# The last half step's raw weight quarters get six tiles of their own, and its token sums get narrower tiles

## The chip, the cores and the metric

The kernel runs on one core of one Trainium2 chip. The metric is device time of one execution in microseconds (us). A core has TensorE (PE, with PEld for its weight loads), VectorE (DVE), ScalarE (ACT), GpSimd (POOL) and SyncE (SP); here SP does nothing but issue DMAs, and POOL issues some DMAs between its vector operations. Each engine takes its instructions in the order in which they were written for it, and an instruction whose inputs or buffer are not ready holds up all that stand behind it on that engine.

## The reference

A backbone of two layers over 512 latent tokens and 256 context tokens of width 1024. Each layer is: a half SwiGLU feed-forward step, a token mixer (neighbourhood attention, then windowed attention), and a second half step. Each part is modulated, gated and closed by a layer norm. All four half steps compute the same formula, with a hidden width of 2816:

```
def swiglu(u, w_in, w_out):
    a, v = jnp.split(u @ w_in, 2, axis=-1)
    return (jax.nn.silu(a) * v) @ w_out

def ffn_sublayer(h, shift, scale, gate, w_in, w_out, g, b):
    y = swiglu(modulate(h, shift, scale), w_in, w_out)
    return layer_norm(ALPHA * h + FFN_RES * gate * y, g, b)
```

In the last half step of the last layer the context tokens are no longer needed, so it runs on the 512 latent tokens alone. That is the half step of this change; the code calls it `1b`.

## The kernel before

**Precision.** A matrix product is made of three fp32r matmuls: each operand is split into a high part and a low part (high x high, low x high, high x low; `mm3`, lines 163, 165 and 166). A weight tile of 128 x 512 comes from memory raw (`wr`), ACT copies it into its high part `wh` (line 102), and POOL or DVE subtracts to get the low part `wl` (line 104). High and low parts of a half step's weights live in a ring of eight tiles each (`RING = 8`), so a new pair can be written only when TensorE is done with the pair eight back.

**A half step.** The hidden width is cut into eleven chunks of 256. A chunk has two weight units of w_in (128 columns of a and 128 of v each) and one unit of w_out. In the middle eight chunks a w_in unit is not multiplied plainly: `seven` multiplies its four quarters in Strassen's manner with seven products instead of eight, over pairs of 128-column token blocks. For that the unit is read as four raw quarters, `wr..00`, `wr..01`, `wr..10` and `wr..11` (a11, a12, a21, a22; `raw_quarter`, line 94 issues the load on SP). POOL makes four sums of them, `S_1` to `S_4` (line 645), each of 128 x 512. Seven pairs of high and low parts follow: for a11, a12 and a22 straight from the quarters (`wh_a`, `wl_a`), for the four sums `wh_s`, `wl_s`. In half step `1b` (where the code's `nb` is 2) DVE makes the low parts of a11, a12, a22 and S_3, POOL those of S_2, S_1 and S_4.

The token side of the products is prepared once per half step: `sums` makes three sums of token blocks for each of four rows and writes their high and low parts to the tiles `T..h` and `T..l` (lines 606 and 607). TensorE then writes the products `p0` to `p6` to PSUM banks; DVE combines them (line 675, tiles `y`), ACT applies silu and copies the high part of the result (`gh`, line 679), and DVE makes its low part (`gl`). The banks of `p5` and `p6` come free with the `gl` operations.

**The w_out unit lags.** A chunk's w_out unit (`lagging`) is multiplied one unit later than its own chunk: TensorE runs the second unit of chunk n, the first unit of chunk n+1, the w_out product of chunk n (`pd`, eight blocks of 128 outputs, accumulated into `z` by DVE at line 504), the second unit of chunk n+1, and so on. There are seven such w_out products in `1b` within the stretch of seven-product units. The low part of a lagging weight is made without a vector subtraction: ACT writes minus the high part (line 108) and a DMA issued by POOL adds the raw weight from memory on top (line 109, `wl_0b` to `wl_3b`).

**Tiles.** Before the change, quarters and the raw tiles of lagging units come from one ring of five (`tag="wr"`, `RAWS = 5`, 2 KB per partition each), in program order. The tiles `T` and two of the `y` tiles are 384 columns wide in every half step, and in `1b` only 256 of them are used (`n2`).

**Order.** The kernel is written with a scheduler that puts the instructions of each engine in an order from its own model of times, when the kernel is built; then the order is fixed. A change to which tile an instruction waits for can therefore move instructions on any engine.

Of the kernel before, what the change touches and what calls it, by code (L numbers as in the profile page):

```python
# [8 lines left out]
F32 = mybir.dt.float32  # L9
F32R = mybir.dt.float32r  # L10
# [7 lines left out]
P = 128  # L18
# [14 lines left out]
RAWS = 5  # L33
# [4 lines left out]
def hybrid_kernel(ctx: ExitStack, tc: tile.TileContext, h0, cc, crow, wmod, wmodt, bmod, lnp, wst,  # L38
# [4 lines left out]
    wp = ctx.enter_context(tc.tile_pool(name="wp", bufs=1))  # L43
# [5 lines left out]
    def bank(tag, nm):  # L49
        return pp.tile([P, 512], F32, tag=tag, name=nm, bufs=banks[tag])  # L50

    def t2(nm, tag="t2"):
        return tp.tile([P, 512], F32, tag=tag, name=nm, bufs={"t2": 6, "ln": 2, "sl": 2}[tag])
# [35 lines left out]
    def flat_or_tiles(t, src):  # L89
        return t[:] if len(src.shape) == 2 else t[:].rearrange("p (k c) -> p k c", c=P)  # L90

    def raw_quarter(src, nm):
        raw = wp.tile([P, 512], F32, tag="wr", name=f"wr{nm}", bufs=RAWS)
        loaded[0] = nc.sync.dma_start(flat_or_tiles(raw, src), src)
        return raw

# [14 lines left out]
    ph, phase_of, slabs_kept = {}, [None, ExitStack()], [SLABS]  # L111
# [397 lines left out]
    def ffn(nm, groups, gt, mid, post, units=(), opened={}, head=None, apart=None):  # L509
# [45 lines left out]
        nb = groups[-1][1] // 256  # L555
        n2 = nb * P
# [13 lines left out]
        def op(eng, out, a, b, o):  # L570
            a, b = [half(y[0], y[1]).bitcast(F32) if isinstance(y, tuple) else as_half(y) for y in (a, b)]
            x = eng.tensor_tensor(out=as_half(out), in0=a, in1=b, op=o)
            if paced:
                behind(x, last_gate[0] if opened else last[0])
# [7 lines left out]
        def sums(j, pool=False):  # L582

            if not paced:
                if not kept_x:
                    kept_x.extend(bank(t, f"x{nm}_{t}") for t in "to")
                b = kept_x[j % 2]
                x1 = (kept_x[0][:, 0:n2], kept_x[1][:, 0:n2], kept_x[1][:, 0:n2], t2(f"x{nm}_{j}_0")[:, 0:n2])[j]
                x2 = (b[:, 256:512] if j < 2 else b[:, 0:256])
                x2s.append(x2)  # L590
            else:
                x1, x2 = [t2(f"x{nm}_{j}_{i}")[:, 0:n2] if pool else bank("s", f"x{nm}_{j}_{i}")[:, 0:n2] for i in range(2)]
            eng = nc.gpsimd if pool else nc.vector
            x3 = t2(f"x{nm}_{j}_2")[:, 0:n2]
            k = j + 4
            op(eng, x1, (uh[j], 1), (uh[j], 0), ALU.subtract)
            op(eng, x1, x1, (ul[j], 1), ALU.add)
            op(eng, x1, x1, (ul[j], 0), ALU.subtract)
            op(nc.gpsimd, x3, (uh[k], 1), (uh[j], 1), ALU.subtract)
            op(nc.gpsimd, x3, x3, (ul[k], 1), ALU.add)  # L600
            op(nc.gpsimd, x3, x3, (ul[j], 1), ALU.subtract)
            op(eng, x2, (uh[k], 1), x1, ALU.subtract)
            op(eng, x2, x2, (ul[k], 1), ALU.add)
            for i, x in enumerate((x1, x2, x3)):
                hi, lo = [ph["T"].tile([P, 384], F32R, tag=f"T{i}{j}{y}", name=f"T{nm}_{i}_{j}{y}", bufs=1)[:, 0:n2] for y in "hl"]
                nc.scalar.copy(hi, x)
                y = nc.vector.tensor_tensor(out=lo, in0=x, in1=hi.bitcast(F32), op=ALU.subtract)
                if paced:
                    behind(y, last_gate[0] if opened else last[0])
                ts[i][j] = [as_half(hi), as_half(lo)]  # L610
# [26 lines left out]
        def quarters(u):  # L637

            src = wst[u].rearrange("p (k c) -> p k c", c=256)
            a11, a12, a21, a22 = [raw_quarter(src[:, h * 4:h * 4 + 4, m * P:m * P + P], f"{u}_{m}{h}")  # L640
                                  for m in range(2) for h in range(2)]

            def tt(n, a, b, o):
                t = t2(f"S{u}_{n}")
                nc.gpsimd.tensor_tensor(out=t[:], in0=a[:], in1=b[:], op=o)  # L645
                return t

            def pair(n, src):
                hi, lo = ring_pair(f"{u}_{n}")
                split_w(hi, lo, src, eng=nc.vector if nb == 2 and n in ("a11", "a12", "a22", "s3") else nc.gpsimd,  # L650
                        y=evacuated[0])
                return hi, lo

            out = [pair("a11", a11), pair("a12", a12)]
            s1 = tt(1, a21, a22, ALU.add)
            s2 = tt(2, s1, a11, ALU.subtract)
            out += [pair("s2", s2), pair("s1", s1)]
            s4 = tt(4, a12, s2, ALU.subtract)
            s3 = tt(3, a11, a21, ALU.subtract)
            return out + [pair("s4", s4), pair("s3", s3), pair("a22", a22)]  # L660

        def seven(un, u, gh, gl):
# [17 lines left out]
                op(half(gl, h), as_half(v), half(gh, h).bitcast(F32), ALU.subtract)  # L680

            sa, sb = [t2(f"y{un}_{i}", "sl")[:, 0:n2] for i in range(2)]
            va, vb = [ph["T"].tile([P, 384], F32, tag=f"y{i}", name=f"y{i}{un}", bufs=2 - i)[:, 0:n2] for i in range(2)]
            nc.scalar.copy(va, product(0, b11))
            tick()
            op(sa, product(1, b21), va)
# [109 lines left out]
        u = wpos[0]  # L796
# [766 lines left out]
```

## Time and profile before

| what | value |
|---|---|
| median of three runs | 2715.3 us (2712.52 to 2730.1) |
| the profiled execution: time, span | 2717.3 us, 2715.5 us |
| busy share of the span: PE, PEld, DVE, ACT, POOL | 97%, 88%, 67%, 44%, 61% |
| granted TensorE clock, mean of the profiled execution | 0.993 |
| the stretch of seven-product units of `1b` | about 2400 to 2632 us of the span |

Busy time is the time in which an instruction of the engine ran; waiting is not in it. Rows of a timeline give the start and the duration in us, the engine, the line of the source, the operation with its written and read tiles, and in brackets how long the engine had been idle before it and what ended that wait. The chain of waits goes back from the last instruction, at each step to what released it. A name's buffer number is left out in the profile, so `S` stands for all four sums, `wr` for any raw quarter, and `pd1b` for the eight blocks of the w_out product of `1b`. In rows of order, the number in a name is the weight unit: in the text below 138 is the second unit of a chunk, 139 that chunk's w_out unit, 140 the first unit of the next chunk, 141 its second.

### The profile page before, as it was taken

The numbers are of one execution on the slowest core, as the hardware profiler recorded it, in microseconds if no ns is written. First come the engines' busy times: TensorE is split into PE (matmuls) and PEld (weight loads), VectorE is DVE, ScalarE is ACT, GpSimd is POOL, SyncE is SP. The second block draws the span as 40 slices with busy tenths as digits, with TensorE's granted clock in tenths as the row PEclk, the third lists the DMA queues.
The fourth block names the chain that finished last, engine by engine and source line by source line (L and its number), as shares of the span: only waits on it lengthen the run. The fifth ranks groups of instructions, "written<-read, shape, count | busy, mean of one in ns | idle before, by whom it ended". The sixth has DMA issues, their size and how long they took to land.

```text
span 2715.5 us, 47718 instructions
## 1 busy us (share of the span) xinstructions
PE 2624.7 (97%) x16858; PEld 2399.9 (88%) x16858; DVE 1828.9 (67%) x4268; ACT 1207.2 (44%) x2505; POOL 1659.6 (61%) x1515
## 2 busy tenths in 40 slices
PE   8999999999999999999999999999999998899997
PEld 5899998888888899999998889999988776899997
DVE  4977778775545686555565776666677767677765
ACT  5334343266455453443433534343337655544542
POOL 4786766455433666867574668676645545667762
PEclk9999999999999999999999999999999999999998
DMA  9367465422211122454543225556642111235551
GB/s 333 100 178 208 137 166 142 147 78 80 59 59 52 50 80 67 129 136 119 133 127 99 75 78 148 143 137 189 178 139 63 32 32 47 71 98 129 143 142 55
DMA packets 294606, 310.85 MB, mean 114 GB/s; under 512 B 27744, under 2 KB 192864, under 8 KB 293344
## 3 DMA queue, kind: packets, MB, share of 16 engines
q1 hardware_dynamic: 277952, 278.31, 33.9%
q0 software_dynamic: 16128, 29.37, 6.4%
q8 instruction: 133, 2.18, 0.3%
q14 instruction: 105, 0.86, 0.1%
q10 hardware_dynamic: 288, 0.14, 0.0%
HBM read 299.87 MB, written 12.25 MB: 115 GB/s over the span
## 4 chain that ended last, share of the span: by engine, by line
PE 83%; DVE 9%; ACT 3%; DMA 2%; issue 2%; POOL 1%; DVEq 0%; SPq 0%; ACTq 0%; POOLq 0%
PE pd1a L163 2%; PE pd1a L165 2%; PE pd1a L166 2%; PE pd0b L163 2%; PE pd0b L165 2%; PE pd0b L166 2%; PE pd0a L163 2%; PE pd0a L165 2%; PE pd0a L166 2%; DVE z L504 1%; PE wo L911 1%; PE pd1b L163 1%; PE o L911 1%; DMA wr<-in_wst_dram 1%; PE pd1b L165 1%
## 5 line engine op out<-in xcount | busy, mean ns | idle before, releaser
L104 POOL TENSOR_TENSOR wl<-wr,wh 128x512 fp32r<-128x512 f32 x200 | 261.1, 1323 | 149.8 <-ACT wh L102 80.0
L104 POOL TENSOR_TENSOR wl_s<-S,wh_s 128x512 fp32r<-128x512 f32 x240 | 316.3, 1355 | 41.6 <-ACT wh_s L102 41.2
L102 ACT CAST wh_s<-S 128x512 fp32r<-128x512 f32 x256 | 155.7, 621 | 413.5 <-POOL S L645 143.2
L645 POOL TENSOR_TENSOR S<-wr,wr 128x512 f32<-128x512 f32 x128 | 173.4, 1355 | 205.4 <-DMA wr<-in_wst_dram 177.7
L212 DVE CUSTOM_DVE_ANT_0 jk<-wt,cb 128x512 f32<-128x512 f32 x360 | 244.4, 679 | 22.9 <-DMA wt<-in_wmodt_dram 18.8
L104 POOL TENSOR_TENSOR wl_a<-wr,wh_a 128x512 fp32r<-128x512 f32 x144 | 190.6, 1371 | 16.4 <-ACT wh_a L102 13.0
L102 ACT CAST wh_a<-wr 128x512 fp32r<-128x512 f32 x192 | 118.7, 622 | 151.3 <-PE pd1b L165 20.9
L102 ACT CAST wh<-wr 128x512 fp32r<-128x512 f32 x200 | 121.2, 617 | 101.2 <-DMA wr<-in_wst_dram 19.5
L504 DVE SCALAR_TENSOR_TENSOR z<-pd0b,gt,z 128x256 f32<-128x256 f32 (+1 forms) x168 | 97.0, 594 | 43.7 <-PE pd0b L166 41.7
L504 DVE SCALAR_TENSOR_TENSOR z<-pd1a,gt,z 128x512 f32<-128x512 f32 (+1 forms) x150 | 88.2, 604 | 31.5 <-PE pd1a L166 24.1
L920 POOL TENSOR_SCALAR p<-p,l 128x512 f32<-128x512 f32 x64 | 44.3, 694 | 104.7 <-DVE l L1034 93.5
L504 DVE SCALAR_TENSOR_TENSOR z<-pd0a,gt,z 128x512 f32<-128x512 f32 (+1 forms) x160 | 94.0, 612 | 16.9 <-PE pd0a L166 16.6
L645 POOL TENSOR_TENSOR S<-wr,S 128x512 f32<-128x512 f32 x64 | 90.4, 1413 | 3.5
L645 POOL TENSOR_TENSOR S<-S,wr 128x512 f32<-128x512 f32 x64 | 90.3, 1411 | 3.1
L920 POOL TENSOR_SCALAR pw<-pw,l 128x512 f32<-128x512 f32 (+1 forms) x64 | 42.6, 666 | 71.1 <-DVE l L1260 41.3
L340 POOL TENSOR_SCALAR z<-z,ag_None,ab_None 128x256 f32<-128x256 f32 (+1 forms) x69 | 53.0, 773 | 48.6 <-DVE uh L325 31.3
L1033 ACT ACTIVATE p<-s,m 128x512 f32<-128x512 f32 x64 | 43.9, 688 | 74.4 <-DVE m L1030 70.1
L326 DVE TENSOR_TENSOR ul<-ufl,uh 128x256 fp32r<-128x256 f32 (+1 forms) x88 | 55.7, 639 | 7.1 <-ACT uh L321 4.1
L319 ACT ACTIVATE ufl<-z,bi_None,sc_None 128x256 f32<-128x256 f32 (+1 forms) x77 | 48.1, 637 | 25.3 <-DVE z L489 24.7
L504 DVE SCALAR_TENSOR_TENSOR z<-pd1b,gt,z 128x512 f32<-128x512 f32 (+1 forms) x91 | 53.1, 617 | 9.0 <-PE pd1b L166 6.2
L163 PE MATMUL vn<-wh,uh 128*128 128x256 f32 x192 | 54.6, 284 | 1.0 <-DVE nq L863 0.6
L104 DVE TENSOR_TENSOR wl_a<-wr,wh_a 128x512 fp32r<-128x512 f32 x48 | 51.7, 1088 | 5.3 <-ACT wh_a L102 5.3
(1483 smaller groups left out, 10565.1 us busy)
## 6 DMA issues: line engine op xcount, KB each, us to landing
wr<-in_wst_dram SPq DMA_DIRECT2D x456, 256.0 KB
wt<-in_wmodt_dram SPq DMA_DIRECT2D x206, 256.0 KB
wr_0b<-in_wst_dram SPq DMA_DIRECT2D x47, 256.0 KB
wr_1b<-in_wst_dram SPq DMA_DIRECT2D x47, 256.0 KB
wr_2b<-in_wst_dram SPq DMA_DIRECT2D x47, 256.0 KB
wr_3b<-in_wst_dram SPq DMA_DIRECT2D x47, 256.0 KB
wm<-in_wmod_dram SPq DMA_DIRECT2D x8, 1024.0 KB
zspare<-in_wmodt_dram SPq DMA_DIRECT2D x30, 256.0 KB
```

Of the source, the lines that this page charges most:

```text
L102: nc.scalar.copy(hi[:], src[:])
L104: x = eng.tensor_tensor(out=lo[:], in0=src[:], in1=hi[:].bitcast(F32), op=ALU.subtract)
L163: behind(nc.tensor.matmul(ps, a[0], b[0], start=first, stop=False), in_front[0])
L165: nc.tensor.matmul(ps, a[0], b[1], start=False, stop=False)
L166: last_pe[0] = nc.tensor.matmul(ps, a[1], b[0], start=False, stop=last)
L212: x = nc.vector.tensor_tensor_reduce(out=junk[:], in0=w[:], in1=cb[st], scale=1.0, scalar=0.0, op0=ALU.mult, op1=ALU.add, accum_out=out[st])
L326: return hi, nc.vector.tensor_tensor(out=lo, in0=uv, in1=uo.bitcast(F32), op=ALU.subtract)
L340: nc.gpsimd.tensor_scalar(out=zs, in0=zs, scalar1=prm[2][:, d:d + 1], scalar2=prm[3][:, d:d + 1], op0=ALU.mult, op1=ALU.add)
L504: last[0] = nc.vector.scalar_tensor_tensor(out=zt(d, c0, c1), in0=pd, scalar=gt[:, d, st:st + 1], in1=zt(d, c0, c1), op0=ALU.mult, op1=ALU ...
L645: nc.gpsimd.tensor_tensor(out=t[:], in0=a[:], in1=b[:], op=o)
L911: last_pe[0] = nc.tensor.matmul(po[64 * h:64 * h + 64, :], t[h][0], t[h][1], start=i == 0, stop=i == len(terms) - 1)
L920: nc.gpsimd.tensor_scalar(out=p, in0=p, scalar1=r, scalar2=0.0, op0=ALU.mult, op1=ALU.add)
```

## The change

In half step `1b` alone, the quarters of the seven-product units no longer come from the ring of five: they take six tiles of their own, in the pool of the phase, and the ring of five is left to the w_out units (and to what comes before and after that stretch). The tiles `T` and `y` are allotted as wide as they are used (`n2`: 256 columns in `1b`, 384 in the others as before). No operation, shape or transfer is added or taken away.

```diff
-    def raw_quarter(src, nm):
-        raw = wp.tile([P, 512], F32, tag="wr", name=f"wr{nm}", bufs=RAWS)
+    def raw_quarter(src, nm, own=None):
+        if own is None:
+            raw = wp.tile([P, 512], F32, tag="wr", name=f"wr{nm}", bufs=RAWS)
+        else:
+            raw = own.tile([P, 512], F32, tag="wr", name=f"wr{nm}", bufs=6)
         loaded[0] = nc.sync.dma_start(flat_or_tiles(raw, src), src)
         return raw
...
-                hi, lo = [ph["T"].tile([P, 384], F32R, tag=f"T{i}{j}{y}", name=f"T{nm}_{i}_{j}{y}", bufs=1)[:, 0:n2] for y in "hl"]
+                hi, lo = [ph["T"].tile([P, n2], F32R, tag=f"T{i}{j}{y}", name=f"T{nm}_{i}_{j}{y}", bufs=1)[:] for y in "hl"]
...
-            a11, a12, a21, a22 = [raw_quarter(src[:, h * 4:h * 4 + 4, m * P:m * P + P], f"{u}_{m}{h}")
+            a11, a12, a21, a22 = [raw_quarter(src[:, h * 4:h * 4 + 4, m * P:m * P + P], f"{u}_{m}{h}",
+                                              ph["T"] if nb == 2 else None)
...
-            va, vb = [ph["T"].tile([P, 384], F32, tag=f"y{i}", name=f"y{i}{un}", bufs=2 - i)[:, 0:n2] for i in range(2)]
+            va, vb = [ph["T"].tile([P, n2], F32, tag=f"y{i}", name=f"y{i}{un}", bufs=2 - i)[:] for i in range(2)]
```

Outside `1b` the order of every engine is unchanged, and within it ACT's order is unchanged. POOL, SP, PE and DVE have instructions in other places. On POOL, between the sums of unit 140 and the low parts of unit 141, this stands before the change:

```order
L104 TENSOR_TENSOR wl140_s2_28315<-S140_2_28312,wh140_s2_28314 128x512
L104 TENSOR_TENSOR wl140_s1_28319<-S140_1_28310,wh140_s1_28318 128x512
L104 TENSOR_TENSOR wl140_s4_28327<-S140_4_28322,wh140_s4_28326 128x512
L109 DMA wl139_0b_28452<-in_wst_dram 128x512
L109 DMA wl139_1b_28459<-in_wst_dram 128x512
L109 DMA wl139_2b_28466<-in_wst_dram 128x512
L109 DMA wl139_3b_28473<-in_wst_dram 128x512
L645 TENSOR_TENSOR S141_1_28557<-wr141_10_28545,wr141_11_28547 128x512
L645 TENSOR_TENSOR S141_2_28559<-S141_1_28557,wr141_00_28541 128x512
L645 TENSOR_TENSOR S141_4_28569<-wr141_01_28543,S141_2_28559 128x512
L645 TENSOR_TENSOR S141_3_28571<-wr141_00_28541,wr141_10_28545 128x512
```

In the changed kernel POOL has the same eleven instructions in this order (the lines are three or four further down in its source):

```order
L107 TENSOR_TENSOR wl140_s2_28315<-S140_2_28312,wh140_s2_28314 128x512
L649 TENSOR_TENSOR S141_1_28557<-wr141_10_28545,wr141_11_28547 128x512
L107 TENSOR_TENSOR wl140_s1_28319<-S140_1_28310,wh140_s1_28318 128x512
L649 TENSOR_TENSOR S141_2_28559<-S141_1_28557,wr141_00_28541 128x512
L107 TENSOR_TENSOR wl140_s4_28327<-S140_4_28322,wh140_s4_28326 128x512
L649 TENSOR_TENSOR S141_4_28569<-wr141_01_28543,S141_2_28559 128x512
L649 TENSOR_TENSOR S141_3_28571<-wr141_00_28541,wr141_10_28545 128x512
L112 DMA wl139_0b_28452<-in_wst_dram 128x512
L112 DMA wl139_1b_28459<-in_wst_dram 128x512
L112 DMA wl139_2b_28466<-in_wst_dram 128x512
L112 DMA wl139_3b_28473<-in_wst_dram 128x512
```

The four sums of unit 141 have moved ahead of the four adding DMAs of unit 139, and between the low parts of unit 140. On SP, the loads of one chunk stand like this before the change:

```order
L94 DMA wr138_10_28139<-in_wst_dram 128x4x128
L94 DMA wr138_11_28141<-in_wst_dram 128x4x128
L94 DMA wr140_00_28294<-in_wst_dram 128x4x128
L94 DMA wr140_01_28296<-in_wst_dram 128x4x128
L94 DMA wr140_10_28298<-in_wst_dram 128x4x128
L94 DMA wr140_11_28300<-in_wst_dram 128x4x128
L94 DMA wr139_0b_28449<-in_wst_dram 128x512
L94 DMA wr139_1b_28456<-in_wst_dram 128x512
L94 DMA wr139_2b_28463<-in_wst_dram 128x512
L94 DMA wr139_3b_28470<-in_wst_dram 128x512
L94 DMA wr141_00_28541<-in_wst_dram 128x4x128
L94 DMA wr141_01_28543<-in_wst_dram 128x4x128
```

and in the changed kernel like this:

```order
L97 DMA wr138_10_28139<-in_wst_dram 128x4x128
L97 DMA wr138_11_28141<-in_wst_dram 128x4x128
L97 DMA wr140_00_28294<-in_wst_dram 128x4x128
L97 DMA wr140_01_28296<-in_wst_dram 128x4x128
L97 DMA wr139_1b_28456<-in_wst_dram 128x512
L97 DMA wr140_10_28298<-in_wst_dram 128x4x128
L97 DMA wr139_2b_28463<-in_wst_dram 128x512
L97 DMA wr139_3b_28470<-in_wst_dram 128x512
L97 DMA wr142_0b_28855<-in_wst_dram 128x512
L97 DMA wr140_11_28300<-in_wst_dram 128x4x128
L97 DMA wr141_00_28541<-in_wst_dram 128x4x128
L97 DMA wr141_01_28543<-in_wst_dram 128x4x128
```

The w_out loads have moved ahead of the last quarter of unit 140, the one of the next chunk's w_out unit (142) among them. On PE the eight blocks of a w_out product are taken in the order 0, 1, 2, 3, 4, the first matmul of 6, 5, the rest of 6, 7 instead of 0, 1, 2, 3, 6, 4, 5, 7; on DVE the accumulations follow that, and one of them moves behind a `gl` operation.

## The prediction

> **What bounds the kernel now.** I read the page first, for which engine fills the span, then the stretch of seven-product units by itself (its busy times, and its waits by engine), then the chain of waits inside it, and last the timelines of POOL, DVE and TensorE over one chunk.
>
> ```profile
> span 2715.5 us, 47718 instructions
> PE 2624.7 (97%) x16858; PEld 2399.9 (88%) x16858; DVE 1828.9 (67%) x4268; ACT 1207.2 (44%) x2505; POOL 1659.6 (61%) x1515
> ...
> 2400.00:2632.00 232.00, 228.19 (x1589) 212.11 (x1588) 167.78 (x282) 114.70 (x235) 167.54 (x131) 1.00 0.54 132
> ...
> PE pd1b L163 <- DVE gl1b L675: 3.8, 3, 2.0
> POOL S L645 <- DMA wr<-in_wst_dram: 36.4, 12, 7.5
> ACT wh_s L102 <- POOL S L645: 53.3, 18, 9.0
> ```
>
> TensorE fills 97% of the span. In the 232.0 us that the change touches it is busy for 228.19 at a granted clock of 1.00 (the columns are span, then PE, PEld, DVE, ACT, POOL, clock, DMA share, GB/s). The difference is 3.8 us, and the waits of TensorE there are the same 3.8 us: three waits of the w_out product for a `gl` operation. POOL waits 36.4 us for raw quarters and ACT 53.3 us for the sums made of them, but almost all of that lies beside a busy TensorE. So the most that this stretch can give is 3.8 us of 2715, or 0.14%.
>
> How the three waits come about is seen in the chain, here at the longest of them:
>
> ```profile
> 2421.80 10.12 DMA wr<-in_wst_dram
> 2432.07 1.28 POOL S L645
> 2433.42 1.30 POOL S L645
> 2434.97 0.30 issue
> 2435.27 0.61 ACT wh_s L102
> 2435.88 0.28 ACT gh1b L679
> 2436.19 0.43 DVE gl1b L675
> 2436.66 0.50 PE pd1b L163
> ```
>
> A raw quarter lands 10.12 us after its issue, POOL makes two sums, ACT copies their high parts, and only then comes the copy `gh`, which stands behind them in ACT's order though it needs no sum. With `gl` a PSUM bank comes free, and the w_out product goes on. The 10 us of the transfer cost TensorE 2.0 us here (the longest of the three).
>
> In the chunk that the rest of this text follows, the same link of the chain is this:
>
> ```profile
> 2486.46 8.51 DMA wr<-in_wst_dram
> ```
>
> **What the change takes away.** Two units fill eight quarters in a chunk. In the ring of five a quarter of unit 141 waits for tiles that w_out unit 139 still holds, so its load goes out only after ACT has made that unit's parts, at 2486.46 in that chunk, and lands 8.51 us later amid the four adding DMAs. With six own tiles the last two quarters of a unit take the tiles of the first two quarters of the unit before: `wr141_10` and `wr141_11` follow `wr140_00` and `wr140_01`, which are free when POOL has made S140_4 and S140_3 and DVE has made the low parts of those two quarters. That is about ten microseconds earlier, and ahead of the adding DMAs. The sums of 141 are then made before the adding DMAs of 139, ACT no longer stops, and the three waits go: **minus 3.8 us**. They were covered by nothing (TensorE stood), so they count in full, if nothing else is late there.
>
> **What is late next.** The order on POOL says what: the four sums of unit 141 now stand ahead of the four adding DMAs of 139, which TensorE needs sooner.
>
> ```profile
> 2476.34 1.75 POOL L645 TENSOR_TENSOR S<-wr,wr 128x512 f32<-128x512 f32 x1
> 2478.06 4.25 POOL L104 TENSOR_TENSOR wl_s<-S,wh_s 128x512 fp32r<-128x512 f32 x3
> 2483.72 0.88 POOL L109 DMA_DIRECT2D wl_0b<-in_wst_dram  x1 [1.40 <-ACT gh1b L679]
> 2488.32 0.86 POOL L109 DMA_DIRECT2D wl_3b<-in_wst_dram  x1 [0.73 <-ACT wl_3b L108]
> 2495.11 1.28 POOL L645 TENSOR_TENSOR S<-wr,wr 128x512 f32<-128x512 f32 x1 [5.93 <-DMA wr<-in_wst_dram]
> ...
> DMA to landing us min/median/max: 4.9/5.7/6.1
> ...
> 2492.15 0.40 PE L163 MATMUL pd1b<-gh1b,wh_0b 128*128 128x512 f32 x1
> 2492.62 0.40 PE L166 MATMUL pd1b<-gh1b,wl_0b 128*128 128x512 f32 x1
> 2495.42 0.40 PE L166 MATMUL pd1b<-gh1b,wl_1b 128*128 128x512 f32 x1
> ```
>
> This is the chunk whose w_out unit is 139 in the order. The adding DMA of `wl_0b` is issued at 2483.72, lands 4.9 to 6.1 us later (median 5.7 of the seven in this stretch), and TensorE first wants `wl_0b` at 2492.62. So before the change there are about 3.2 us to spare (2492.62 less 2483.72 less 5.7). How much later the issue is now follows from a chain that starts at TensorE:
>
> ```profile
> 2473.69 0.62 ACT L102 CAST wh_a<-wr 128x512 fp32r<-128x512 f32 x1 [0.93 <-PE p01b L165]
> 2474.10 2.83 DVE L104 TENSOR_TENSOR wl_a<-wr,wh_a 128x512 fp32r<-128x512 f32 x2
> 2488.63 0.69 DVE L104 TENSOR_TENSOR wl_a<-wr,wh_a 128x512 fp32r<-128x512 f32 x1 [0.15 <-ACT wh_a L102]
> ...
> 2637.05 3.41 DMA wr_0b<-in_wst_dram
> ...
> 2478.55 0.38 SPq L94 DMA_DIRECT2D wr_2b<-in_wst_dram  x1
> 2479.03 0.38 SPq L94 DMA_DIRECT2D wr_3b<-in_wst_dram  x1
> ...
> L104 POOL TENSOR_TENSOR wl_s<-S,wh_s 128x512 fp32r<-128x512 f32 x45 | 63.2, 1431 | 1.2 <-ACT wh_s L102 1.2
> L645 POOL TENSOR_TENSOR S<-wr,wr 128x512 f32<-128x512 f32 x29 | 41.1, 1418 | 36.6 <-DMA wr<-in_wst_dram 36.4
> ```
>
> - *Start.* The high part of `wr140_01` can be written when product p0 of unit 138 frees its place in the ring; that copy ends at 2474.31. Its low part on DVE ends 0.69 us later if POOL is quiet (2475.0), or at 2476.93 as in this trace, where POOL's sums ran beside it. I take 2476.0. POOL must also be done with S140_3; it ended at 2478.09 here, and comes earlier with the change, since the four sums of 138 no longer stand behind the adding DMAs.
> - *Load.* A raw load with little beside it takes 3.41 us, one amid the adding DMAs took 8.51. At that time those of the last chunk are done, so 3.4: `wr141_11` lands at about 2479.4.
> - *POOL.* From there six vector operations stand ahead of the DMA of `wl_0b`: S141_1, wl140_s1, S141_2, wl140_s4, S141_4, S141_3. At 1.42 us each that is 8.5 us, so it is issued at 2487.9 instead of 2483.72.
> - *Landing.* Plus 5.7: 2493.6. TensorE wants it at 2492.62: **a new wait of about 1.0 us**, at each of the seven w_out products, 7.0 us in all.
>
> Both ends of this: if DVE is quick (2475.0), the load takes 3.4, POOL's six operations 1.28 us each as in the row at 2495.11 and the landing 4.9, the part is there at 2491.0 and there is no wait. If S140_3 is as late as before (2478.1), the load of `wr141_10` goes ahead of `wr141_11` (0.5, the step between two issues on SP at 2478.55 and 2479.03), POOL takes 1.42 and the landing 6.1, it is there at 2496.6, a wait of 4.0 us. I take 1.0 since the middle rows of each step lead there. The wait does not grow from chunk to chunk: the chain starts anew at each chunk from a product of TensorE. The other three adding DMAs follow a microsecond apart and are wanted 2.8 us (2495.42 less 2492.62) and more after the first, so the first decides.
>
> The Trainium skill's page "DMA: Bandwidth & Descriptors", section "Anatomy of one DMA — SWDGE (gpsimd) path", gives a DMA issued by POOL about 2.0 us plus its bytes over 436 GB/s, by which 256 KB take an estimated 2.6 us; no new wait would arise, and the time would be the 2711.5 of the first rival. The landing row of this trace, 4.9 us at the least, speaks against it: these DMAs add onto what stands in the tile, and share the engines with raw loads.
>
> **Edits that cost nothing.** Narrower `T` and `y` tiles change no operand's shape (the 256 columns were used before too); they make the room for the six tiles. On SP the loads of w_out unit 142 now stand ahead of the last quarter of unit 143. They take tiles that ACT leaves between 2483.4 and 2487.8, when it has made the parts of 139; that quarter follows `wr141_01`, whose low part DVE ends at 2490.8, so nothing is held up. If something were, one load of 8.51 us would stand in the way, and POOL has 9.6 us of the chunk free (21.66 of 31.30 busy). ACT's order is the same, DVE's moved accumulations free banks that TensorE asks for later, and the order of the w_out blocks costs TensorE no matmul.
>
> ```profile
> 2482.79 0.63 ACT L108 ACTIVATE wl_0b<-wr_0b 128x512 fp32r<-128x512 f32 x1
> 2487.15 0.63 ACT L108 ACTIVATE wl_3b<-wr_3b 128x512 fp32r<-128x512 f32 x1
> 2490.07 0.69 DVE L104 TENSOR_TENSOR wl_a<-wr,wh_a 128x512 fp32r<-128x512 f32 x1 [0.15 <-ACT wh_a L102]
> ...
> 2472.00:2503.30 31.30, 30.88 (x216) 28.53 (x215) 21.10 (x36) 15.65 (x32) 21.66 (x18) 1.00 0.54 130
> ```
>
> **The sum.** The profiled execution took 2717.3 us (span 2715.5). Less 3.8, plus 7.0: 2720.5. It lies 2.0 us above the median of the runs, 2715.3, so against that median the forecast is about **2719 us** (2718.5): no change that can be measured. A measurement of this kernel tells about 1% (27 us) from no change.
>
> **The rivals.**
>
> *No new wait* (25%). The adding DMA lands in time, by the quick end above, and the three waits go: 2715.3 less 3.8 is 2711.5. For it: the seven landings are within 1.2 us of each other, and I may overrate POOL by a microsecond. Against it: all six POOL operations must run at their shortest, while DVE makes low parts beside them.
>
> *The wait is long* (25%): slower. Here POOL's six operations are stretched by DVE, and the chain begins as late as S140_3 did. The row of 1.75 us at 2476.34, where DVE ran its two low parts (1.41 each, against 0.69 alone), shows the stretch: six at 1.75 are 10.5, 2.0 more than in my sum, so 3.0 us a product, 7 x 3.0 less 3.8 = plus 17.2, or 2732. With the late start as well (2478.1 instead of 2476.0) it is 5.1 us, plus 32, or 2747. Every wait over 0.54 us a product makes the change slower than before (3.8 / 7), and from 4.4 us on ((27 + 3.8) / 7) it is over 1%. Against it: POOL's free 9.6 us let it be early at the chain's start. The Trainium skill's page "SBUF — State Buffer", section "Who interferes with whom", has DVE and GpSimd share a port pair under an exclusive lock, so that the later one waits for the other's whole instruction. By that rule each POOL operation could be held by one DVE combination; at 0.42 us each (an estimate from rows like the `gl` of 0.43 above) that is 2.5 us a product, and with my 1.0 the sum is 2736; I give it 5 of the 25 parts. The trace agrees in that both sides slow down, but not in the size: 0.72 more on DVE and 0.45 more on POOL are each less than the other's whole instruction.
>
> *The change does not do what it says* (3%). If raw loads are late for another reason than tiles (the DMA engines are 54% busy in this stretch), the sums of 141 come as late as now, and the adding DMAs of 139 stand behind them. POOL would then begin at 2495.11, issue `wl_0b` 8.5 us later, and it would land at 2509.3, a wait of 16.7 us a product: about 2828. It is the dearest case and has little for it, since the load at 2637.05 shows 3.4 us without neighbours.
>
> **Chances and range.** The forecast (a wait of 0.3 to 1.8 us a product, minus 1.7 to plus 8.8 us, 2713.6 to 2724.1) has 46%. Outside 1% upwards lie the last rival and the far part of the long wait, together 6%; downwards nothing reaches it, because TensorE's waits in this stretch sum to 3.8 us: 1% for what I don't see. That leaves 93% within 1%. The range takes in the forecast, the case without a wait and most of the long one: 2709 (2711.5 less the 2.8 us by which the lowest run lies under the median) to 2732.
>
> **What would show it.** In the changed kernel's profile, POOL's wait of `S` for raw quarters falls from 36.4 us to under 20, ACT's for `S` from 53.3 to under 15, and TensorE no longer waits for `gl` at `pd1b`. If I am right on the new wait, TensorE waits at `pd1b` line 166 (169 there) for the DMA of `wl_0b`, seven times, about a microsecond each; if the first rival is, it waits there not at all. TensorE waits of over 4 us there, or raw quarters that still land 8 us after their issue ahead of the sums, would prove the forecast wrong.

## The result, and the profile after

The changed kernel takes **2729.9 us** (median of 11 runs, 2723.2 to 2741.1), the kernel before 2715.3: the ratio is 1.0047, with a 95% interval of 1.0034 to 1.0060. It is slower by half a per cent, where the forecast was no change that can be measured. It lies 11 us above the forecast of 2719 and outside the 2713.6 to 2724.1 that had 46%, but inside the range.

The profiled execution took 2723.2 us (span 2721.4), the shortest of its eleven, so the sum is better made in the stretch that the change touches. It is taken here from the first matmul of product `p0` of the second seven-product unit to the first matmul behind the last one. Its start lies elsewhere in each execution; the length is the first number behind the bounds, followed by PE, PEld, DVE, ACT, POOL, granted clock, DMA share and GB/s. Before:

```profile
2407.46:2640.63 233.17, 229.36 (x1598) 213.28 (x1597) 165.96 (x279) 113.73 (x234) 166.66 (x130) 1.00 0.54 133
```

After:

```profile
2398.95:2646.67 247.72, 234.59 (x1599) 215.98 (x1597) 159.04 (x280) 116.80 (x233) 164.25 (x130) 0.98 0.49 119
```

The stretch is 14.5 us longer (247.7 less 233.2), close to the 14.6 between the medians. Two numbers grew: the time in which TensorE is idle (3.8 us before, 13.1 now) and, unexpectedly, its busy time, by 5.2 us at a granted clock of 0.98. The waits of the changed kernel in this stretch:

```profile
POOL S L649 <- DMA wr<-in_wst_dram: 49.6, 10, 7.1
ACT wh_s L105 <- PE pd1b L168: 44.1, 14, 6.2
...
PE pd1b L169 <- DMA wl_0b<-in_wst_dram: 12.9, 7, 3.1
PE pd1b L169 <- DMA wl_1b<-in_wst_dram: 0.2, 1, 0.2
```

TensorE no longer waits for `gl`. It waits at each of the seven w_out products for the adding DMA of `wl_0b`, 12.9 us in all, 1.8 on average. ACT's long waits for `S` are gone (what is left is the wait for TensorE to leave a place in the ring), but POOL's wait for raw quarters rose from 36.4 to 49.6.

POOL's timeline in the chunk that the prediction followed (its w_out product starts at 2487.28 here, 4.87 us earlier in the span than before):

```profile
2468.79 1.76 POOL L649 TENSOR_TENSOR S<-wr,wr 128x512 f32<-128x512 f32 x1
2470.98 1.30 POOL L107 TENSOR_TENSOR wl_s<-S,wh_s 128x512 fp32r<-128x512 f32 x1 [0.43 <-ACT wh_s L105]
2475.59 1.49 POOL L649 TENSOR_TENSOR S<-wr,wr 128x512 f32<-128x512 f32 x1 [3.31 <-DMA wr<-in_wst_dram]
2477.04 1.75 POOL L107 TENSOR_TENSOR wl_s<-S,wh_s 128x512 fp32r<-128x512 f32 x1
2478.76 1.30 POOL L649 TENSOR_TENSOR S<-S,wr 128x512 f32<-128x512 f32 x1
2480.02 1.29 POOL L107 TENSOR_TENSOR wl_s<-S,wh_s 128x512 fp32r<-128x512 f32 x1
2481.28 1.30 POOL L649 TENSOR_TENSOR S<-wr,S 128x512 f32<-128x512 f32 x1
2482.55 1.31 POOL L649 TENSOR_TENSOR S<-wr,wr 128x512 f32<-128x512 f32 x1
2483.81 0.80 POOL L112 DMA_DIRECT2D wl_0b<-in_wst_dram  x1
...
2496.68 1.35 POOL L649 TENSOR_TENSOR S<-wr,wr 128x512 f32<-128x512 f32 x1 [6.87 <-DMA wr<-in_wst_dram]
```

S140_3 ends at 2470.55. The loads for unit 141 follow it; POOL waits 3.31 us for them and begins S141_1 at 2475.59; six operations later, at 2483.81, the adding DMA goes out, 3.5 us ahead of the product that needs it. Before the change the lead was 8.4 us (2483.72 against 2492.15). The landing takes as long as before:

```profile
DMA to landing us min/median/max: 5.8/5.9/6.1
```

Where the busy time grew is seen in four of the seven w_out products, each from its first matmul to the next unit's first. Undisturbed, this work takes 11.20 us:

```profile
2418.98:2434.18 15.20, 12.87 (x51) 10.12 (x50) 8.87 (x14) 3.13 (x6) 8.06 (x7) 0.89 0.68 152
...
2487.28:2500.80 13.52, 11.55 (x50) 8.86 (x49) 8.01 (x14) 3.13 (x6) 6.65 (x6) 1.00 0.74 165
2520.83:2536.75 15.92, 12.87 (x51) 10.09 (x50) 8.65 (x14) 3.13 (x6) 8.94 (x8) 0.89 0.69 152
2556.75:2568.96 12.21, 11.52 (x51) 8.86 (x49) 8.02 (x14) 3.13 (x6) 6.04 (x5) 1.00 0.71 160
```

Three of the seven (the two here and a third of 15.35) ran at a granted clock of 0.89. TensorE's timeline at the longest wait shows it; the columns are start, duration and, in brackets, the wait:

```profile
2524.51 0.68 PE L169 MATMUL pd1b<-gh1b,wl_0b 128*128 128x512 f32 x1 [3.05 <-DMA wl_0b<-in_wst_dram]
2524.99 0.63 PE L166 MATMUL pd1b<-gh1b,wh_0b 128*128 128x512 f32 x1
2525.41 0.63 PE L168 MATMUL pd1b<-gl1b,wh_0b 128*128 128x512 f32 x1
...
2528.26 0.39 PE L169 MATMUL pd1b<-gh1b,wl_0b 128*128 128x512 f32 x1
2528.49 0.40 PE L166 MATMUL pd1b<-gh1b,wh_1b 128*128 128x512 f32 x1
```

For 3.5 us behind the wait a matmul starts every 0.42 us; from 2528.26 on, every 0.23. Of the product's 15.92 us, 11.20 are work, 3.05 the wait, and 1.67 the low clock. The three products with a low clock lose 5.1 us in this way (15.20 + 15.92 + 15.35, less 3 x 11.20, less the waits of 2.33, 3.05 and 2.35).

### The profile page after: what moved, and what is told of

The parts are those of the page before. It is cut to its first block, busy times and chain, and to the rows that moved or that the text cites. A ratio compares the mean times of both kernels' runs of the same rounds, so it can differ in the third digit from the quotient of the medians.

```text
span 2721.4 us, 47700 instructions
## 1 busy us (share of the span) xinstructions
PE 2628.1 (97%) x16858; PEld 2399.9 (88%) x16858; DVE 1812.4 (67%) x4268; ACT 1210.7 (44%) x2505; POOL 1659.4 (61%) x1515
## 4 chain that ended last, share of the span: by engine, by line
PE 82%; DVE 9%; DMA 3%; ACT 3%; issue 2%; POOL 1%; DVEq 0%; ACTq 0%; POOLq 0%
PE pd0b L166 2%; PE pd0b L168 2%; PE pd1a L168 2%; PE pd0b L169 2%; PE pd1a L166 2%; PE pd1a L169 2%; PE pd0a L168 2%; PE pd0a L166 2%; PE pd0a L169 2%; PE pd1b L169 1%; DMA wl_0b<-in_wst_dram 1%; PE pd1b L166 1%; DVE z L507 1%; PE pd1b L168 1%; PE wo L915 1%
## 5 line engine op out<-in xcount | busy, mean ns | idle before, releaser
L107 POOL TENSOR_TENSOR wl_a<-wr,wh_a 128x512 fp32r<-128x512 f32 x144 | 190.5, 1371 | 14.6 <-ACT wh_a L105 11.4
L168 PE MATMUL vn<-wl,uh 128*128 128x256 f32 x192 | 54.3, 283 | 0.0
```

The source lines that it names most:

```text
L107: x = eng.tensor_tensor(out=lo[:], in0=src[:], in1=hi[:].bitcast(F32), op=ALU.subtract)
L168: nc.tensor.matmul(ps, a[0], b[1], start=False, stop=False)
```

## The experiments

**The order on POOL alone.** The question is whether the loss comes from the four sums that stand ahead of the adding DMAs. An ordering of POOL puts them behind again; the six tiles stay, and SP's loads follow. TensorE and DVE then take the order of the kernel before again too, so this run alone does not tell POOL's order from that of the w_out blocks. The run with eight tiles below does: it keeps the changed order of TensorE and DVE, and loses nothing.

```diff
...
-            nc.gpsimd.dma_start(flat_or_tiles(lo, mem), mem, accum_op=ALU.add)
+            adding_dma[0] = nc.gpsimd.dma_start(flat_or_tiles(lo, mem), mem, accum_op=ALU.add)
...
-                nc.gpsimd.tensor_tensor(out=t[:], in0=a[:], in1=b[:], op=o)
+                x = nc.gpsimd.tensor_tensor(out=t[:], in0=a[:], in1=b[:], op=o)
+                if nb == 2 and n == 1:
+                    behind(x, adding_dma[0])
```

> The changed kernel, but POOL is told to issue the four adding DMAs of w_out before the first sum of the next second unit (an order on POOL alone; the six own tiles stay). Theory (the loss is that these sums stand ahead of the adding DMAs on POOL): the seven waits for wl_0b, 13.1 us, are gone, and with them the stretches at a low granted clock after them, some 5 us. Whether the three waits for gl (3.8 us) come back is open: if the raw quarters are there early, they do not, and the time is 2711 to 2713; if they do, 2715. Rival (more raw loads in flight slow the adding DMAs, or something else in the tiles): the landing of wl_0b and the waits for it stay, 2727 to 2732.

Measured: 2710.0 us, against 2716.1 of the kernel before; ratio 0.9965 (0.9947 to 0.9984). It is faster than both kernels. Its stretch, by the same bounds:

```profile
2420.66:2649.26 228.60, 228.60 (x1598) 213.71 (x1597) 166.61 (x279) 116.73 (x233) 166.78 (x130) 1.00 0.52 129
```

TensorE is busy for every one of the 228.60 us, 19.1 us less than in the changed kernel and 4.6 less than before. Its POOL in one chunk (the w_out product starts at 2503.14):

```profile
2486.85 4.13 POOL L107 TENSOR_TENSOR wl_s<-S,wh_s 128x512 fp32r<-128x512 f32 x3 [1.86 <-ACT wh_s L105]
2494.72 0.89 POOL L112 DMA_DIRECT2D wl_0b<-in_wst_dram  x1 [3.74 <-ACT gh1b L685]
2496.69 0.86 POOL L112 DMA_DIRECT2D wl_1b<-in_wst_dram  x1 [1.09 <-ACT wl_1b L111]
...
2499.31 0.86 POOL L112 DMA_DIRECT2D wl_3b<-in_wst_dram  x1 [0.72 <-ACT wl_3b L111]
2499.88 1.63 POOL L649 TENSOR_TENSOR S<-wr,wr 128x512 f32<-128x512 f32 x1
```

The adding DMA goes out 8.4 us ahead of the product, as before the change, and the sum behind the last one finds its raw quarters there: it starts without a wait, where before the change it had waited 5.93 us. So the six tiles do what they were expected to do for the `gl` waits; it is the order on POOL that took more away than they gave.

**The narrower tiles alone.** The raw quarters stay in the ring of five.

```diff
-                                              ph["T"] if nb == 2 else None)
+                                              None)
```

> Only the second half of the change: token sums in tiles of 256 columns, the raw quarters in the common ring of five as before. Theory: nothing there moves; 2713 to 2718, waits for gl 3 to 4 us at the w_out products, none for wl_0b. Rival (the narrower tiles, lying elsewhere in memory, slow DVE or POOL): at least a third of the loss, over 2719.

Measured: 2724.7 us, ratio 1.0017 (0.9998 to 1.0036). The median lies where the rival had put it, over 2719, but the interval takes in no change. In the profile the stretch takes 234.3 us, 1.1 more than before, and its waits are of the kind of the kernel before.

```profile
PE pd1b L166 <- DVE gl1b L679: 5.0, 4, 1.6
```

There is no wait for `wl_0b`. In this execution the rest lies ahead of the stretch, which starts 7.4 us later than before (2414.88 against 2407.46): up to there the two kernels have the same instructions in the same order, but the granted clock is 0.992 instead of 0.996. The fastest kernel of this study has the narrow tiles too. No cost of theirs can be seen in the profile; the times alone don't exclude one of some microseconds.

**More and fewer own tiles.** First eight instead of six.

```diff
-            raw = own.tile([P, 512], F32, tag="wr", name=f"wr{nm}", bufs=6)
+            raw = own.tile([P, 512], F32, tag="wr", name=f"wr{nm}", bufs=8)
```

> The changed kernel with eight own tiles instead of six. The last quarter of the second unit still follows S3 of the first on POOL, but only one load stands in its way instead of two to four. Theory (POOL's chain from S3 of the first unit over a load and six operations to the adding DMA): the load lands about 1 us earlier, so each wait is some 1 us shorter: 13.1 falls to about 6 us, no wait over 2.3 us and so no low clock: 2716 to 2720. Rival (the number of loads in flight is what costs): the waits are as long or longer, 2728 or more.

Measured: 2713.0 us, ratio 0.9980 (0.9962 to 0.9997); the stretch takes 228.8 us and TensorE waits for neither `wl_0b` nor `gl` there. I had forecast that half the waits would stay. POOL's timeline shows why they don't (the product starts at 2489.87):

```profile
2466.82 1.32 POOL L649 TENSOR_TENSOR S<-wr,wr 128x512 f32<-128x512 f32 x1 [2.11 <-DMA wr<-in_wst_dram]
2468.22 1.77 POOL L649 TENSOR_TENSOR S<-S,wr 128x512 f32<-128x512 f32 x1
...
2478.76 1.77 POOL L649 TENSOR_TENSOR S<-wr,wr 128x512 f32<-128x512 f32 x1
2481.44 0.89 POOL L112 DMA_DIRECT2D wl_0b<-in_wst_dram  x1 [0.91 <-ACT wl_0b L111]
```

The sums of unit 141 still stand ahead of the adding DMA, but S141_1 begins 23.1 us ahead of the product instead of 11.7, because the sums of unit 140 are done earlier too: S140_3 ends by 2464.7 (2466.82 less 2.11), 25.2 us ahead of the product instead of 16.7. More tiles move both units' loads, not only the last one. The scheduler chose another order on POOL here too (seven operations from S141_1 to the adding DMA, one more than with six tiles), and still POOL comes to the adding DMA 0.91 us before ACT is ready for it. The order on POOL costs nothing if the quarters are there in time.

Then five:

> The changed kernel with five own tiles instead of six. The last quarter of the second unit now takes a tile that DVE leaves one low part later, and the second of its loads waits for the last low part of the unit before. Theory (too few tiles set the start of POOL's chain, and the order on POOL carries it to the adding DMAs): the sums start later, waits for wl_0b longer than with six, 15 to 28 us in all, 2735 to 2750. Rival (the waits come from more raw loads in flight): fewer in flight with five, shorter waits than with six, under 2727.

Measured: 2732.5 us, ratio 1.0055 (1.0030 to 1.0081), a stretch of 248.2 us, and about the same waits as with six:

```profile
PE pd1b L169 <- DMA wl_0b<-in_wst_dram: 13.5, 7, 4.0
```

The expectation (15 to 28 us) was missed. The scheduler chose another order for five: one low part fewer stands between S141_1 and the adding DMA, which makes up for sums that begin 2 us later against the product. The rival (fewer loads in flight, shorter waits) fell too.

**The length of POOL's chain.** Two of the six operations, the low parts of S_1 and S_4, are given to DVE.

```diff
-        split_w(hi, lo, src, eng=nc.vector if nb == 2 and n in ("a11", "a12", "a22", "s3") else nc.gpsimd,
+        split_w(hi, lo, src, eng=nc.vector if nb == 2 and n in ("a11", "a12", "a22", "s3", "s1", "s4") else nc.gpsimd,
```

> The changed kernel with the low parts of the sums s1 and s4 made by DVE instead of POOL, so that four POOL operations instead of six stand between the last raw quarter and the adding DMA of wl_0b, which is issued some 2.8 us earlier. The order (sums ahead of the adding DMAs) and the six tiles stay. Theory (a chain of POOL operations): the waits of 0.7 to 3.05 us shrink by 2.8 us each, to under 1 us in all, no low clock after them; the stretch from the first product of the seven-product units to the last one's end is some 238 us instead of 256, the time 2711 to 2714, unless DVE's four more operations a chunk make gl late (up to 4 us more). Rival (the landing among more loads is what is late): the waits stay over 10 us, 2727 or more.

Measured: the waits of TensorE for `wl_0b` and `wl_1b` shrink to 1.3 us, the clock in the stretch is 1.00 and its length 231.1 us.

```profile
PE pd1b L169 <- DMA wl_0b<-in_wst_dram: 0.7, 2, 0.5
PE pd1b L169 <- DMA wl_1b<-in_wst_dram: 0.6, 2, 0.4
```

The time, 2718.8 us, is above the 2711 to 2714 expected; its ratio, 0.9989 (0.9963 to 1.0014), lies clearly under that of the changed kernel and cannot be told from 1. By the stretch it should be 2 us under the kernel before, which that interval holds.

In the other direction, one more POOL operation ahead of the adding DMA of `wl_0b`; the scheduler then also put the DMA of `wl_1b` ahead of it.

```diff
...
+            if first and "T" in ph:
+                extra = ph["T"].tile([P, 512], F32, tag="extra", name="extra", bufs=1)
+                nc.gpsimd.tensor_tensor(out=extra[:], in0=lo[:].bitcast(F32), in1=lo[:].bitcast(F32), op=ALU.add)
             nc.gpsimd.dma_start(flat_or_tiles(lo, mem), mem, accum_op=ALU.add)
...
```

> The changed kernel with one more POOL operation of 1.4 us ahead of the adding DMA of wl_0b, which also goes out second of the four (0.55 us): it is issued some 2.0 us later. Its result goes nowhere. Theory: each of the seven waits grows by 2.0 us, 13.1 to about 27 us, and if a wait over 2.3 us makes TensorE run at half clock for a few us after it (1.7 us each), that now happens at all seven instead of three: 2729.9 plus 14 plus 4 times 1.7, about 2751. If the low clock has nothing to do with the length of the wait: 2744. Rival (the adding DMA is late for another reason than POOL's order, its place in the transfers): no growth, 2730 to 2733.

Measured: 2740.6 us, ratio 1.0079 (1.0050 to 1.0109), where the changed kernel has 1.0047 (1.0034 to 1.0060): the intervals overlap, so the time alone does not tell the two apart. The waits do.

```profile
PE pd1b L172 <- DMA wl_1b<-in_wst_dram: 19.9, 6, 5.5
PE pd1b L172 <- DMA wl_0b<-in_wst_dram: 1.7, 4, 0.6
```

The waits grow from 13.1 to 21.6 us, less than the 27 expected, and TensorE waits for another tile: the scheduler had interleaved matmuls of the next unit with the w_out product, so this run shows the direction and not the size.

**The landing.** POOL makes the low parts of w_out itself, and no DMA adds.

```diff
-                w = wunit(again=u, adding=True)
+                w = wunit(again=u, adding=nb == 3)
```

> The changed kernel, but POOL makes the low parts of w_out itself (raw quarter less its high part, 1.4 us each) instead of issuing DMAs that add the quarter onto its negative; order and tiles as changed. It takes the landing out of the chain: wl_0b is there 1.4 us after POOL comes to it, instead of some 5.8 us after. Theory: no wait for wl_0b at all, some 3.5 us more work for POOL in each chunk that its idle time takes up, 2710 to 2714. If POOL's work is the bound rather than the landing: waits for wl_0b made by POOL of about 1 us each, 2720 or more.

Measured: 2714.4 us, ratio 0.9987 (0.9969 to 1.0005), a stretch of 230.7 us. The only wait of TensorE left in it is

```profile
PE pd1b L166 <- DVE gl1b L679: 1.7, 2, 1.0
```

With the same order on POOL and six tiles, the wait for `wl_0b` is gone when its landing is. The run takes away more than the landing, though: with no adding DMAs beside the loads, POOL waits 29.1 us for raw quarters instead of 49.6. It does not tell the two apart.

**The changed kernel again**, in another execution.

> The changed kernel once more, beside the two below, to see whether its waits come back in the same place and size in another execution. Theory: seven waits for wl_0b of 0.7 to 3.1 us, 11 to 15 us in all, and a low granted clock behind those of over 2 us and not behind the others; 2726 to 2734. If the waits were an accident of one execution, they are spread otherwise or gone.

Measured: 2733.8 us, ratio 1.0056 (1.0039 to 1.0073), a stretch of 246.2 us.

```profile
PE pd1b L169 <- DMA wl_0b<-in_wst_dram: 13.9, 7, 3.2
PE pd1b L169 <- DMA wl_1b<-in_wst_dram: 0.6, 2, 0.4
```

The waits come back chunk by chunk: 2.10, 1.91, 2.27, 3.23, 0.65, 2.23 and 1.54 us, against 2.33, 1.69, 1.73, 3.05, 0.69, 2.35 and 1.05. The low clock does not: only the product behind the wait of 3.23 us has it, not those behind 2.27 and 2.23.

**The price of a wait.** Three kernels start from the one with the adding DMAs first, hold TensorE and the adding DMAs to the order in which they are written, and put four, five or seven POOL operations ahead of each adding DMA of `wl_0b`. TensorE's order is the same in all three; from that of the kernel they start from it differs in the place of one block of each w_out product, and once in the two first products of a unit. The lines that make them:

```diff
...
+            for _ in range(extra):
+                t = ph["T"].tile([P, 512], F32, tag="extra", name="extra", bufs=1)
+                nc.gpsimd.tensor_tensor(out=t[:], in0=lo[:].bitcast(F32), in1=lo[:].bitcast(F32), op=ALU.add)
...
```

> To price a wait by itself: the kernel with the adding DMAs first (237.3 us in this stretch, no waits), the order of TensorE and of the four adding DMAs held, and four POOL operations (1.04 us each, results unused) ahead of each adding DMA of wl_0b. It had some 2.8 us to spare, so TensorE should wait about 1.4 us at each of seven w_out products. If only a wait over about 2 us brings the clock down: 9.8 us of waits, granted clock 1.00 in the stretch, stretch 247 us, time about 2720. If any wait does: another 1.65 us each, stretch 259, time 2731.

> The same with five POOL operations ahead of wl_0b: a wait of about 2.4 us at each of seven products, 16.8 us. If a wait over about 2 us brings the clock to a half for some 3.5 us: 1.65 us more each, stretch 266 us, time about 2738. If the clock has nothing to do with it: stretch 254, time 2727.

> The same with seven POOL operations ahead of wl_0b: a wait of about 4.5 us at each of seven products, 31.5 us. With 1.65 us of low clock behind each: stretch 280 us, time about 2753; if a longer wait brings a longer stretch at half clock, more than that; without any: 269, time 2741.

| extra operations | waits for `wl_0b`, us | longest | stretch, us | more than 228.6, less the waits | time, us (ratio, interval) |
|---|---|---|---|---|---|
| 4 | 9.9 | 1.7 | 239.0 | 0.5 | 2720.1 (1.0008, 0.9988 to 1.0029) |
| 5 | 9.6 | 2.1 | 240.5 | 2.3 | 2722.9 (1.0030, 1.0012 to 1.0048) |
| 7 | 26.5 | 4.0 | 270.7 | 15.6 | 2753.4 (1.0124, 1.0097 to 1.0151) |

With waits of 0.98 to 1.66 us (four operations) the granted clock stays 1.00 and a wait costs its own length. With seven, all seven waits are 3.6 to 4.0 us, and every product behind one runs at a low clock; the stretch, and two of the products:

```profile
2404.36:2675.11 270.75, 244.20 (x1599) 223.87 (x1598) 157.37 (x279) 116.96 (x233) 216.70 (x179) 0.92 0.44 109
```

```profile
2461.11:2477.71 16.60, 12.86 (x51) 10.11 (x49) 8.97 (x14) 3.74 (x7) 16.24 (x14) 0.90 0.55 111
2497.72:2515.15 17.43, 13.62 (x50) 10.68 (x49) 8.55 (x13) 3.75 (x7) 17.05 (x15) 0.80 0.53 106
```

The first lost 1.7 us beside its wait (16.60 less 11.20, less 3.74), the second 2.4 (17.43 less 11.20, less 3.81), against 1.65 in my expectation. The run with five operations missed the 2.4 us a wait that I had expected: the landing of an adding DMA that is issued later is shorter. From issue to landing (the last number, the median), with four operations and with seven, the latter for six of the seven:

```profile
wl_0b<-in_wst_dram POOLq DMA_DIRECT2D x7, 256.0 KB, 5.9
```

```profile
wl_0b<-in_wst_dram POOLq DMA_DIRECT2D x6, 256.0 KB, 4.3
```

With five it is 4.8, 1.1 less, which takes back the 1.04 us of the fifth operation. That the loads issued at the same time have then drained is what I take for the reason; no run separates it.

## Why the prediction was right or wrong, point by point

- **The waits for `gl` go.** Right: none is left in the changed kernel, and their 3.8 us come off the time where nothing takes their place. The kernel with the adding DMAs first gains 4.6 us in the stretch.
- **The adding DMA stands behind four sums, and `wl_0b` is late at each of seven products.** Right in place, sign and number: seven waits at line 169. Putting the sums behind again, starting them early with eight tiles, shortening the chain by two operations, and taking out the landing each removed nearly all of the waits.
- **Which tiles follow which.** Wrong in the name. I had `wr141_10` and `wr141_11` follow the first two quarters of unit 140, with the chain starting at a low part on DVE. In the built kernel the tiles rotate otherwise: `wr141_01` takes the tile of `wr140_10`, free when POOL has made S140_3, and on SP, which issues in order, `wr141_10` and `wr141_11` stand behind it. The start of the chain was well placed, 2470.55 against 2471.1 of the forecast (2476.0 less 4.87), but by luck: the forecast took it from a copy that TensorE releases and a low part on DVE, and it came from POOL's own sum.
- **Start, load, six operations, landing.** In this chunk the load took 4.9 us from the end of S140_3 to its landing (POOL could begin at 2475.59) instead of 3.4, since three loads go out in a row, the last at 2471.55, which lands 3.9 us later; the six operations 8.2 instead of 8.5; the landing 5.8 instead of 5.7. The wait came to 1.73 us instead of 1.0; over the seven it is 1.84 on average. The load is the term that was mis-sized: I priced one load where three are issued.
- **The clock.** Missing from the sum. TensorE ran at half its rate for some 3.5 us behind three of the seven waits, 5.1 us in the profiled execution. The stretch adds up as 13.1 of waits, 5.1 of clock and 0.9 that the other four products lose beside their waits (0.07 to 0.36 each), less the 4.6 that the fastest kernel shows to have been there to gain: plus 14.5, where the forecast had plus 3.2. The terms are not independent of each other, as the next point shows. That the time fell inside the range is in part luck: the range reached to 2732 for stretched POOL operations and a late start, and a low clock, which no case of the forecast had, used that room.
- **The wait does not grow from chunk to chunk.** Right in what it says (2.33 in the first, 1.05 in the last), wrong in its reason: the chain does not start anew at each chunk from a product of TensorE. SP's loads of raw quarters come in bursts, and the first load of each goes out 0.03 us after a sum of POOL has ended: for the second unit after S140_3 (2470.55), for the first unit of the next chunk after S141_3 (2483.86), and so in six chunks of the stretch:

```profile
2470.58 7.45 SPq L97 DMA_DIRECT2D wr<-in_wst_dram  x5
...
2483.89 0.37 SPq L97 DMA_DIRECT2D wr<-in_wst_dram  x1
...
2485.90 1.59 SPq L97 DMA_DIRECT2D wr<-in_wst_dram  x2
```

The load issued at 2485.90 lets POOL go on at 2496.68, which leads to the next S140_3, its burst, and the next S141_3: a circle of POOL and the loads, in which TensorE has no part in this chunk. The adding DMAs of `wl_0b` go out 33.3 to 34.6 us apart over the stretch (34.0 on average), where an undisturbed chunk takes 31.23 (the kernel with the adding DMAs first). What TensorE loses in a chunk, to the wait and the low clock together, is the difference of the two paces, so what the low clock takes is in good part taken off the next wait: the waits behind the three products at a low clock are 1.69, 0.69 and 1.05, the others 1.73 and more. In the second execution of the changed kernel the low clock took 1.7 us instead of 5.1, the waits 14.5 instead of 13.1, and the stretch was only 1.5 us shorter. How far the circle is free of TensorE, two executions don't settle.

- **What would show it.** ACT's wait for `S` went as foretold. POOL's wait for raw quarters was to fall under 20 us and rose to 49.6: the first unit's quarters are now issued together with the adding DMAs and land up to 10.7 us after their issue (POOL waits 6.87 us for them at 2496.68). I had named late quarters ahead of the sums as a sign against the forecast; the sign appeared at the other unit, and it is what holds S140_3, and so the whole chain, where it is. The cover that I gave the moved loads of unit 142 ("nothing is held up") did not see this.
- **The rivals.** The long wait came nearest to the measured time (2732 against 2729.9), but not by its mechanism: POOL's operations were mostly at 1.3 us and not stretched to 1.75, and the sums did not start late. Two of the six, 1.49 and 1.75, ran beside a low part on DVE (from 2475.21 and 2476.69), the other four beside its combinations. The prediction's 2736 had a combination hold each of the six. The Trainium skill's page "SBUF — State Buffer", section "Who interferes with whom", doesn't say that: there a DVE instruction with two inputs in SBUF (a low part) contends with a POOL operation that reads SBUF, and one with at most one such input (a combination, which reads PSUM) does not. The trace agrees: in the stretch of the kernel before, 25 POOL operations beside combinations or accumulations alone took 1.28 to 1.32 us, and 59 beside a low part up to 1.76. By the Trainium skill's page "DMA: Bandwidth & Descriptors", section "Anatomy of one DMA — SWDGE (gpsimd) path", the landing would be an estimated 2.6 us; the shortest that these runs show is 4.2, in the kernels with five and with seven extra operations.

## What to carry to other kernels

When loads get more room, ask which in-order queue their consumers stand in and what they now stand ahead of: work that became ready early can take the place of something short whose result is wanted sooner, and one line that fixes the order kept the gain and removed the loss. Price the last of several loads that are released together, not a single one. Follow the chain of a wait round to where it starts: here it closed on itself through POOL and the loads, and then a wait is the difference of two paces and not a sum of steps. A wait of the busiest engine can cost more than its length, so look at the granted clock of the stretch behind it before a wait goes into a sum.

## What the runs showed of the hardware

**A wait of TensorE can be followed by half rate.** In the w_out products of six profiled executions (the changed kernel twice, five tiles, and the three kernels with extra operations), no wait under 2 us was followed by a granted clock under 1.00, each one from 2.5 us up was, and between them both were seen: 2.33 and 2.35 (the changed kernel) and 2.13 (five extra operations) were, 2.10, 2.23 and 2.27 (the changed kernel again) were not. It costs 1.5 to 2.6 us beside the wait. The traces show what decides. In all 13 profiled executions the granted clock changes only on a grid of 3.41 us, which lies elsewhere against the program in each. Of the intervals of this grid within the stretch that ran at full rate, 17 held 1.93 us or more of idle TensorE, and each was followed by half rate; the other 868 held 1.80 us or less, and none was. The wait of 2.27 us is cut by the grid into 1.40 and 0.87; the one of 2.13 lies in one interval. The Trainium skill's page "TensorE: Matmul & The Clock Gate", section "Part 1: The HAM clock gate", puts the drop to half rate behind an idle time of about 3.4 us, judged in a window that runs on its own; the half rate and the window of its own agree with these runs, but the idle time that was enough here is shorter.

**It is also a good part of what makes executions of one program differ.** In the 13 profiled executions the stretch starts between 2398.95 and 2420.66 us, and the granted clock up to there lies between 0.9986 (in the two earliest) and 0.9894 (in the latest). One execution does not fit (2409.31 with 0.9901), so the clock is not all of it. In an earlier part of the program, the same in both kernels (TensorE has gaps of up to 1.6 us there), an execution of the kernel before has

```profile
2294.00:2331.00 37.00, 30.11 (x243) 25.87 (x242) 28.88 (x92) 23.22 (x58) 22.28 (x28) 1.00 0.15 44
```

and one of the kernel with the adding DMAs first

```profile
2300.00:2342.00 42.00, 35.87 (x240) 31.55 (x238) 28.54 (x89) 23.58 (x58) 22.45 (x28) 0.80 0.15 39
```

The same some 240 matmuls take 5 us more at a clock of 0.80, where several gaps follow one another. The profiled execution of the fastest kernel took 2725.0 us and that of the changed one 2723.2, though the medians are 19.9 us apart the other way; only the stretch, or many runs, tells them apart.
